# Another loading order at the opening of a Hymba step: three tiles of x, all first weights into idle HGRN tiles, then the other x

## Chip, core and metric

One NeuronCore of a Trainium2 chip runs the whole program. The metric is the device time of one execution in microseconds, as a median of several runs; lower is better. TensorE (PE) does matrix products and transposes, VectorE (DVE), ScalarE (ACT) and GpSimd (POOL) elementwise work, and SyncE (SP) issues most transfers; ACT and POOL issue some of them too.

## The reference

One step of a hybrid decoder layer, for a prompt of 1024 tokens and 8 sample tokens that share all weights. Both groups are normalised and multiplied by one wide input projection; its columns feed sparse attention (NSA: compressed, selected and window branches) and an HGRN2 recurrence, and an output projection follows. What matters here is the first part:

```python
def _rmsnorm(x, g):
    x32 = x.astype(jnp.float32)
    y = x32 * lax.rsqrt(jnp.mean(x32 * x32, axis=-1, keepdims=True) + EPS)
    return (y * g.astype(jnp.float32)).astype(x.dtype)

def _project(x, g_pre, w_in):
    z = _split(_rmsnorm(x, g_pre) @ w_in)          # ..., q_b, f_b, i_b, z_b: 512 columns each
    ...

def _hgrn_inputs(z, lb):
    fl = z['f_b'].astype(f32)
    f = lb + (1.0 - lb) * jax.nn.sigmoid(fl)
    k = (1.0 - lb) * jax.nn.sigmoid(-fl)
    q = jax.nn.silu(z['q_b'].astype(f32))
    v = z['i_b'].astype(f32)
    ...
```

`x_prompt` is 1024 x 1024, `x_sample` 8 x 1024, all in float32. The paged caches are found through a `page_table` of 8 x 8 integers.

## The kernel before

**x.** `load_x` (from L178) brings x in as nine tiles of 128 tokens (the ninth holds the 8 sample tokens), 1024 columns each. They lie in tiles that the HGRN part uses later: tiles 0 to 3 share one buffer `V`, tiles 4 to 8 are `x_in`, in the buffers of `AT`, `S` and `O`. L190 issues all nine loads on SP. For each tile, ACT squares it and sums (L200, `x_sq` and `x_ss`), DVE works out the inverse root by bit tricks and three Newton steps of tiny 128x1 operations (L202 and L79 to L84), DVE scales the tile in place (L214), PE transposes it in two halves of four blocks into PSUM `ph` (L218), and each half is split into a rounded part `xhi` (ACT, L50) and the remainder `xlo` (DVE, L51). The statistics of the next tile are written in the code ahead of the scaling of the present one.

**Weights.** `load_w` (from L224) brings in one block of columns of `w_in` as eight parts of 128 rows. Each part goes by L233 into a raw buffer `w_raw`, of which three cycle; ACT writes the rounded, `g_pre`-scaled part `w_hi` (L238) and DVE the remainder `w_lo` (L239); nine buffers of each. The first block has two pieces of 256 columns, so two loads for a part, 16 in all. From the second block to the fifth, `load_w` also issues, behind the loads, two copies of the window cache in DRAM (L244, 0.5 MB each).

**Products.** PE computes three products for a full-precision one: hi by hi, hi by lo, lo by hi (all at L42). The first block gives the features F, K (ACT at L311 and L312, DVE at L313 and L315) and Q (L323, L324) in groups of 344 tokens: a group needs three tiles of x and all eight weight parts. The second block (L329 evacuates it into `V`, by ACT) has 512 columns; the third is 256 columns wide.

**Small loads.** `gpre` (L290), `hgn` (L141) and two `hg_lo` (L145) are issued by ACT; `hg_lo` is tied behind the last x load. `page_index` loads the page table in eight pieces (L648, `pt_raw`); nothing but the order of the list ties seven of them to a place.

**Order.** The code yields operations and a scheduler of the framework puts them into a list for each engine, by a timeline of its own. Each engine works its list off in order. Each DMA that SP or ACT issues carries one of eight completion semaphores in turn, and waits for the DMA eight before it.

Of the kernel before, what the change touches and what calls it, by code (L numbers as in the profile page):

```python
# [7 lines left out]
F32 = mybir.dt.float32  # L8
# [4 lines left out]
AF = mybir.ActivationFunctionType  # L13
OP = mybir.AluOpType
# [7 lines left out]
TS = T + NB  # L22
D = 1024
EPS = 1e-6
C_Q, C_KC, C_KS, C_KW, C_G, C_ZA, C_QB, C_FB, C_IB, C_ZB = 0, 512, 768, 1024, 1280, 1304, 1816, 2328, 2840, 3352


class Kernel:
# [148 lines left out]
    def load_x(self, ctx):  # L177
        nc, a = self.nc, self.a  # L178
        self.xhi = self.xpool.tile([128, 8, TS], F32R, name="xhi")
        self.xlo = self.xpool.tile([128, 8, TS], F32R, name="xlo")  # L180
        wk = self.pool(ctx, "xwork", bufs=2)
        xs, hp = [], self.hp
        four = hp.tile([128, 8, 512], F32, name="V", bufs=1).rearrange("p a b -> p (a b)")
        for i in range(9):
            n = 128 if i < 8 else NB
            if i < 4:
                x = four[:, i * D:(i + 1) * D]
            else:
                x = hp.tile([128, 8, 128], F32, name="x_in", tag=("AT", "S", "O")[(i - 4) // 2]).rearrange("p a b -> p (a b)")[:n]
            self.xdma = nc.sync.dma_start(x, a["x_prompt"][0, i * 128:i * 128 + n] if i < 8 else a["x_sample"][:, 0])  # L190
            xs.append((i, n, x))

        def norms(tiles):
            ss = wk.tile([128, 4], F32, name="x_ss")
            if tiles[-1] == 8:
                nc.gpsimd.memset(ss, 1.0)
            for j, t in enumerate(tiles):
                _, n, x = xs[t]
                junk = wk.tile([128, D], BF, name="x_sq")[:n]
                nc.scalar.activation(junk, x, AF.Square, accum_out=ss[:n, j:j + 1])  # L200
            ss = ss[:, :len(tiles)]
            nc.vector.tensor_scalar(ss, ss, 1.0 / D, EPS, op0=OP.mult, op1=OP.add)  # L202
            r = wk.tile([128, 4], F32, name="x_rs")[:, :len(tiles)]
            self.rsqrt(wk, r, ss)
            return r

        groups = [(i,) for i in range(9)]
        r = norms(groups[0])
        for gi, tiles in enumerate(groups):
            rn = norms(groups[gi + 1]) if gi + 1 < len(groups) else None  # L210
            for j, t in enumerate(tiles):
                i, n, x = xs[t]
                tok = slice(i * 128, i * 128 + n)
                nc.vector.tensor_scalar(x, x, r[:n, j:j + 1], None, op0=OP.mult)  # L214
                for h in range(2):
                    p = self.ps_h.tile([128, 512], F32, name="ph").rearrange("p (a b) -> p a b", a=4)
                    for k in range(4):
                        nc.tensor.transpose(p[:, k, :n], x[:, (4 * h + k) * 128:(4 * h + k + 1) * 128], self.ident[:n, :n])  # L218
                    self.split(self.xhi[:, 4 * h:4 * h + 4, tok], self.xlo[:, 4 * h:4 * h + 4, tok], p[:, :, :n],
                               nc.scalar, nc.vector)  # L220
            r = rn
            yield gi

    def load_w(self, src, *parts):  # L224

        nc = self.nc
        out = []
        width = sum(p[1] for p in parts)
        for k in range(8):
            raw = self.wpool.tile([128, 512], F32, name="w_raw", bufs=3)[:, :width]  # L230
            o = 0
            for c0, n in parts:
                dma = nc.sync.dma_start(raw[:, o:o + n], src[k * 128:(k + 1) * 128, c0:c0 + n])  # L233
                o += n
            hi = self.wpool.tile([128, 512], F32R, name="w_hi", bufs=9)[:, :width]
            lo = self.wpool.tile([128, 512], F32R, name="w_lo", bufs=9)[:, :width]
            g = self.gpre[:, k:k + 1]
            nc.scalar.activation(hi, raw, AF.Copy, scale=g)  # L238
            nc.vector.scalar_tensor_tensor(lo, raw, g, hi.bitcast(F32), op0=OP.mult, op1=OP.subtract)  # L239
            out.append((hi, lo))  # L240
        self.nload += 1
        for b in range(2 * self.nload - 4, 2 * self.nload - 2):
            if 0 <= b < NB:
                self.after(nc.sync.dma_start(  # L244
                    self.a["win_kv_sample"][0, b, :511].rearrange("s a h d -> s (a h d)"),
                    self.a["cache_win_kv"][0, b, 1:].rearrange("s a h d -> s (a h d)")), dma)
        return out
# [32 lines left out]
    def project(self, ctx):  # L280
        nc, a = self.nc, self.a
# [5 lines left out]
        hp = self.hp = self.pool(hctx, "hg", bufs=2)  # L287
        with ExitStack() as c:
            self.gpre = self.xpool.tile([128, 8], F32, name="gpre")
            nc.scalar.dma_start(self.gpre, a["g_pre"][0].rearrange("(k p) -> p k", p=128))  # L290
            self.nload = 0
            x = self.load_x(c)
            next(x)
            w0 = self.load_w(a["w_in"][0], (C_FB, 256), (C_QB, 256))
            for _ in x:
                pass
            self.consts2(c, mp)
# [5 lines left out]
        K, Q, F = {}, {}, {}  # L303
# [338 lines left out]
    def page_index(self, pool):  # L642

        nc = self.nc
        pt = self.a["page_table"]
        raw = pool.tile([128, NB], I32, name="pt_raw", bufs=1)
        for i in range(8):
            dma = nc.sync.dma_start(raw[16 * i:16 * i + 16], bass.AP(tensor=pt.tensor, offset=pt.offset + i, ap=[[0, 16], [8, NB]]))  # L648
            if i == 0:
                self.pidma = dma  # L650
        lane = pool.tile([128, NB], I32, name="pt_lane", bufs=1)
        nc.gpsimd.iota(lane, pattern=[[0, NB]], base=0, channel_multiplier=1)
        nc.vector.tensor_scalar(lane, lane, 15, None, op0=OP.bitwise_and)
        self.pidx = self.cp.tile([128, NB], I32, name="pidx")
        nc.vector.scalar_tensor_tensor(self.pidx, raw, 16.0, lane, op0=OP.mult, op1=OP.add)
# [738 lines left out]
```

## Time and profile before

| | us |
|---|---|
| median of 3 runs | 1093.54 |
| lowest, highest run | 1088.66, 1094.07 |
| profiled execution, its own time | 1092.95 |
| its span in the trace | 1091.2 |
| PE busy | 1051.9 |
| DVE, ACT, POOL busy | 618.0, 388.5, 241.1 |

Starts and lengths in the trace count from the start of the span. PE's busy time overlaps with its own weight loads (PEld). An engine's row says in square brackets, or behind the last bar, how long it idled ahead and what ended that. ACTq and SPq are the queues of transfers that these engines issue; a row of them covers from the first issue to the end of the last. The first product of this kernel starts after 20 us, and the stage of the first block ends at about 77 us.

### The profile page before, as it was taken

What the parts mean: (1) busy time and instruction counts of PE and PEld (TensorE: products, weight loads), DVE (VectorE), ACT (ScalarE), POOL (GpSimd) and SP (SyncE); (2) the same over time, 40 slices, a digit from 0 to 9 for tenths busy, and PEclk for the clock granted to TensorE, in tenths of its full rate; (3) what the DMA queues carried; (4) which work ended last, traced back from release to release, by engine and by line L of the source; (5) the groups of instructions that cost most, each with busy time, mean ns of one, the idle gap of its engine ahead of it and who ended that gap; (6) DMA issues with size and microseconds to landing.
All of it is one profiled execution on the core that took longest, in us unless ns stands there. A gap on an engine that the chain in (4) does not pass through costs nothing.

```text
span 1091.2 us, 18921 instructions
## 1 busy us (share of the span) xinstructions
PE 1051.9 (96%) x7021; PEld 936.8 (86%) x7021; DVE 618.0 (57%) x1822; ACT 388.5 (36%) x786; POOL 241.1 (22%) x276
## 2 busy tenths in 40 slices
PE   4999999999899899999989999999999999999998
PEld 3898799999789899999968898888788888778876
DVE  6847565666484535543574666766655677461223
ACT  4622234313133335432224544553554332241112
POOL 0024231331031133002023111111323133131111
PEclk9999999999999999999969999999999999999999
DMA  6212023333454666304468711001831474131110
GB/s 195 78 29 68 11 72 100 117 101 120 144 173 135 193 222 208 135 1 118 123 186 250 189 38 42 20 21 41 230 111 42 137 199 119 41 97 49 47 37 31
DMA packets 119007, 116.44 MB, mean 107 GB/s; under 512 B 18902, under 2 KB 101166, under 8 KB 116612
## 3 DMA queue, kind: packets, MB, share of 16 engines
q1 hardware_dynamic: 97412, 79.46, 25.6%
q10 hardware_dynamic: 19200, 19.01, 5.1%
q0 software_dynamic: 2304, 16.78, 4.6%
q8 instruction: 55, 0.90, 0.4%
q14 instruction: 36, 0.29, 0.1%
HBM read 84.84 MB, written 29.31 MB: 105 GB/s over the span
## 4 chain that ended last, share of the span: by engine, by line
PE 81%; DMA 9%; DVE 5%; issue 2%; ACT 1%; POOL 1%; SPq 0%; ACTq 0%; DVEq 0%; POOLq 0%
PE pa L42 37%; PE pb L42 27%; PE ph L42 9%; PE pt L42 4%; DMA vb<-v_d 2%; DMA w_raw<-w_in 2%; PE ph L714 1%; DMA w1r<-cmp_w 1%; DMA fw_raw<-w_out 1%; PE pa L1124 1%; DMA f_z<-oT_d 1%; DMA cg<-cache_cmp_kv,pidx 1%; DMA V<-x_prompt 1%; PE ph L1318 1%; DVE w_lo L239 1%
## 5 line engine op out<-in xcount | busy, mean ns | idle before, releaser
L42 PEld LDWEIGHTS pb<-V,P 128*128 128x128 f32 x1056 | 143.8, 194 | 11.8 <-POOL P L959 0.9
L42 PE MATMUL pb<-V,P 128*128 128x128 f32 x1056 | 149.2, 279 | 0.5 <-DVE mx L908 0.4
L42 PE MATMUL pa<-xhi,w_hi 128*128 128x344 f32 x384 | 125.7, 329 | 3.3 <-ACT w_hi L238 1.7
L42 PE MATMUL pa<-xlo,w_hi 128*128 128x344 f32 x384 | 124.2, 325 | 0.0
L42 PE MATMUL pa<-xhi,w_lo 128*128 128x344 f32 x384 | 123.3, 326 | 0.0
L954 ACT ACTIVATE P<-ph 128x512 f32<-128x512 f32 (+4 forms) x148 | 85.8, 595 | 100.4 <-PE ph L42 78.3
L915 DVE CUSTOM_DVE_ANT_0 junk<-pa,mask 128x320 bf16<-128x320 f32 (+5 forms) x150 | 73.1, 496 | 35.7 <-PE pa L42 35.1
L42 PE MATMUL pa<-w_lo,xhi 128*128 128x256 f32 (+2 forms) x256 | 79.8, 316 | 0.1
L42 PE MATMUL pa<-w_hi,xlo 128*128 128x256 f32 (+2 forms) x256 | 79.6, 315 | 0.0
L42 PE MATMUL pa<-w_hi,xhi 128*128 128x256 f32 (+2 forms) x256 | 78.9, 317 | 0.0
L42 PEld LDWEIGHTS pa<-xhi,w_hi 128*128 128x128 f32 x384 | 73.3, 191 | 5.0 <-ACT w_hi L238 2.4
L238 ACT ACTIVATE w_hi<-w_raw,gpre 128x512 fp32r<-128x512 f32 (+2 forms) x80 | 47.4, 616 | 78.1 <-DMA w_raw<-w_in 46.5
L42 PEld LDWEIGHTS pa<-xlo,w_hi 128*128 128x128 f32 x384 | 73.2, 191 | 0.1
L42 PEld LDWEIGHTS pa<-xhi,w_lo 128*128 128x128 f32 x384 | 72.7, 190 | 0.4 <-DVE w_lo L239 0.2
L42 PE MATMUL ph<-QA,KA 128*128 128x512 f32 (+4 forms) x148 | 66.4, 451 | 2.5 <-ACT P L954 2.5
L42 PE MATMUL pa<-KB,QB 65*128 65x320 f32 (+6 forms) x195 | 64.8, 369 | 1.1 <-DVE mx L915 0.7
L239 DVE SCALAR_TENSOR_TENSOR w_lo<-w_raw,gpre,w_hi 128x512 fp32r<-128x512 f32 (+2 forms) x80 | 51.4, 663 | 21.6 <-ACT w_hi L238 20.9
L42 PE MATMUL pa<-fw_hi,yh 128*128 128x512 f32 (+1 forms) x160 | 61.7, 385 | 0.0
L42 PE MATMUL pa<-fw_hi,yl 128*128 128x512 f32 (+1 forms) x160 | 61.6, 385 | 0.0
L42 PE MATMUL pa<-fw_lo,yh 128*128 128x512 f32 (+1 forms) x160 | 61.6, 385 | 0.0
L42 PE MATMUL ph<-QB,KB 68*128 68x512 f32 (+3 forms) x148 | 58.5, 405 | 0.0
L42 PE MATMUL pb<-x,w1h 128*128 128x384 f32 (+1 forms) x192 | 55.9, 353 | 0.3 <-ACT x L50 0.3
(457 smaller groups left out, 2391.3 us busy)
## 6 DMA issues: line engine op xcount, KB each, us to landing
w_raw<-w_in SPq DMA_DIRECT2D x32, 256.0 KB
w_raw<-w_in SPq DMA_DIRECT2D x48, 128.0 KB
VS<-sg SPq DMA_DIRECT2D x8, 512.0 KB
sg<-cache_win_kv SPq DMA_DIRECT2D x16, 256.0 KB
fw_raw<-w_out SPq DMA_DIRECT2D x16, 256.0 KB
fw_raw<-ple_gate SPq DMA_DIRECT2D x16, 256.0 KB
f_x<-x_prompt SPq DMA_DIRECT2D x8, 512.0 KB
win_kv_sample<-cache_win_kv SPq DMA_DIRECT2D x8, 511.0 KB
```

The costliest lines, as they stand in the source:

```text
L42: return self.nc.tensor.matmul(out, lhsT, rhs, start=start, stop=stop, skip_group_check=True)
L238: nc.scalar.activation(hi, raw, AF.Copy, scale=g)
L239: nc.vector.scalar_tensor_tensor(lo, raw, g, hi.bitcast(F32), op0=OP.mult, op1=OP.subtract)
L714: nc.tensor.transpose(pt[:, i * 128:(i + 1) * 128], src[b0 + j // 2, kv][:, j % 2, 2 * jp:2 * jp + 2].rearrange("p j d -> p (j d)"), self. ...
L915: nc.vector.tensor_tensor_reduce(junk, pm, mk, 1.0, -1e30, op0=OP.add, op1=OP.max, accum_out=o)
L954: nc.scalar.activation(P, ps, AF.Exp, scale=0.125)
L1124: nc.tensor.transpose(pt[:, j * 128:(j + 1) * 128], rows(j), self.ident)
L1318: nc.tensor.transpose(pt[:, c], h[:, k * 128:(k + 1) * 128], self.ident[:n, :n])
```

## The change

Four edits, all at the opening. The loads: SP issues x tiles 0 to 2, then all 16 pieces of the first weights, then x tiles 3 to 8 (a `yield` in `load_x`). The first weights no longer go through the three raw buffers, but into eight halves of four tiles `w0`, in the buffers of F and K, which are not used until the first products are evacuated. The norms: tiles 1 and 2 share one chain of tiny operations, 128x2 instead of twice 128x1. GpSimd: parts 5 to 7 of the first weights are scaled by POOL in place, copied to `w_hi` by ACT (L50), and subtracted by POOL (L51); DVE and ACT at L247 and L248 do parts 0 to 4 as before. The page table: its loads are tied behind the last weight load issued so far, which is that of the second block.

```diff
@@ load_x
             else:
                 x = hp.tile([128, 8, 128], F32, name="x_in", tag=("AT", "S", "O")[(i - 4) // 2]).rearrange("p a b -> p (a b)")[:n]
+            if i == 3:
+                yield
             self.xdma = nc.sync.dma_start(x, a["x_prompt"][0, i * 128:i * 128 + n] if i < 8 else a["x_sample"][:, 0])
...
-        groups = [(i,) for i in range(9)]
+        groups = [(0,), (1, 2)] + [(i,) for i in range(3, 9)]
@@ load_w
-    def load_w(self, src, *parts):
+    def load_w(self, src, *parts, raws=None):
...
-            raw = self.wpool.tile([128, 512], F32, name="w_raw", bufs=3)[:, :width]
-            o = 0
-            for c0, n in parts:
-                dma = nc.sync.dma_start(raw[:, o:o + n], src[k * 128:(k + 1) * 128, c0:c0 + n])
-                o += n
+            if raws:
+                raw = raws[k]
+            else:
+                raw = self.wpool.tile([128, 512], F32, name="w_raw", bufs=3)[:, :width]
+                o = 0
+                for c0, n in parts:
+                    dma = self.lastw = nc.sync.dma_start(raw[:, o:o + n], src[k * 128:(k + 1) * 128, c0:c0 + n])
+                    o += n
...
-            nc.scalar.activation(hi, raw, AF.Copy, scale=g)
-            nc.vector.scalar_tensor_tensor(lo, raw, g, hi.bitcast(F32), op0=OP.mult, op1=OP.subtract)
+            if raws and k > 4:
+                nc.gpsimd.tensor_scalar(raw, raw, g, None, op0=OP.mult)
+                self.split(hi, lo, raw, nc.scalar, nc.gpsimd)
+            else:
+                nc.scalar.activation(hi, raw, AF.Copy, scale=g)
+                nc.vector.scalar_tensor_tensor(lo, raw, g, hi.bitcast(F32), op0=OP.mult, op1=OP.subtract)
@@ project
             next(x)
-            w0 = self.load_w(a["w_in"][0], (C_FB, 256), (C_QB, 256))
+
+            raws = []
+            for tag in ("F", "F", "K", "K"):
+                t = hp.tile([128, TS], F32, name="w0", tag=tag)
+                raws += [t[:, :512], t[:, 512:1024]]
+            for k, raw in enumerate(raws):
+                for o, c0 in ((0, C_FB), (256, C_QB)):
+                    nc.sync.dma_start(raw[:, o:o + 256], a["w_in"][0, k * 128:(k + 1) * 128, c0:c0 + 256])
+            for _ in range(2):
+                next(x)
+            w0 = self.load_w(None, (C_FB, 256), (C_QB, 256), raws=raws)
             for _ in x:
                 pass
@@ page_index
             dma = nc.sync.dma_start(raw[16 * i:16 * i + 16], bass.AP(tensor=pt.tensor, offset=pt.offset + i, ap=[[0, 16], [8, NB]]))
+            self.after(dma, self.lastw)
```

The scheduler moves more than the diff says. First the list of SP at the opening. `V_126` is the buffer of x tiles 0 to 3, `x_in_131` (before) and `x_in_151` (after) are tile 4, the `x_in` behind them tiles 5 to 7; `w0_130` to `w0_133` each hold two parts of the first weights. Before:

```order
L190 DMA V_126<-x_prompt 128x1024 x4
L190 DMA x_in_131<-x_prompt 128x1024
L190 DMA x_in_133<-x_prompt 128x1024
L190 DMA x_in_135<-x_prompt 128x1024
L190 DMA x_in_137<-x_prompt 128x1024
L190 DMA x_in_139<-x_sample 8x1024
L233 DMA w_raw_192<-w_in 128x256 x2
L233 DMA w_raw_199<-w_in 128x256 x2
L233 DMA w_raw_206<-w_in 128x256 x2
L648 DMA pt_raw_1476<-page_table 16x8x1 x7
L233 DMA w_raw_213<-w_in 128x256 x2
```

And SP at the same place after:

```order
L192 DMA V_126<-x_prompt 128x1024 x3
L310 DMA w0_130<-w_in 128x256 x4
L310 DMA w0_131<-w_in 128x256 x4
L310 DMA w0_132<-w_in 128x256 x4
L310 DMA w0_133<-w_in 128x256 x4
L192 DMA V_126<-x_prompt 128x1024
L192 DMA x_in_151<-x_prompt 128x1024
L192 DMA x_in_153<-x_prompt 128x1024
L192 DMA x_in_155<-x_prompt 128x1024
L192 DMA x_in_157<-x_prompt 128x1024
L192 DMA x_in_159<-x_sample 8x1024
L238 DMA w_raw_1180<-w_in 128x512
```

The loads of x tiles 3 and 4 stand behind sixteen weight loads now; the page table has left the place.

Second, ACT's list from the first `xhi` copies on. A PSUM tile `ph` is half a tile of x: before, `ph_178` and `ph_185` are tile 0, `ph_267` and `ph_274` tile 1, `ph_300` tile 2; `x_in_131` and `x_in_133` are tiles 4 and 5. Before:

```order
L50 CAST xhi_121<-ph_178 128x4x128
L50 CAST xhi_121<-ph_185 128x4x128
L50 CAST xhi_121<-ph_267 128x4x128
L200 ACTIVATE x_sq_315,x_ss_314<-x_in_131 128x1024
L50 CAST xhi_121<-ph_274 128x4x128
L238 ACTIVATE w_hi_195<-w_raw_192,gpre_119 128x512
L200 ACTIVATE x_sq_348,x_ss_347<-x_in_133 128x1024
L150 ACTIVATE hg_ex_510<-hg_ex_510 128x8
L238 ACTIVATE w_hi_202<-w_raw_199,gpre_119 128x512
L50 CAST xhi_121<-ph_300 128x4x128
```

After, from the second half of tile 0 on: `ph_207` is tile 0, `ph_233` and `ph_240` are tile 1, `ph_248` is tile 2; `V_126` in the fourth row is tile 3, `x_in_151` tile 4.

```order
L50 CAST xhi_121<-ph_207 128x4x128
L50 CAST w_hi_282<-w0_132 128x512
L145 DMA hg_lo_488<-hg_lower 128x4x1
L202 ACTIVATE x_sq_215,x_ss_214<-V_126 128x1024
L145 DMA hg_lo_488<-hg_lower 128x4x1
L50 CAST w_hi_287<-w0_133 128x512
L202 ACTIVATE x_sq_298,x_ss_297<-x_in_151 128x1024
L50 CAST xhi_121<-ph_233 128x4x128
L50 CAST w_hi_292<-w0_133 128x512
L50 CAST xhi_121<-ph_240 128x4x128
L50 CAST xhi_121<-ph_248 128x4x128
```

The squares of tiles 3 and 4 stand ahead of all `xhi` copies of tiles 1 and 2 now; before, the square of tile 3 stood ahead of them too, but that of tile 4 behind the first. DVE's list has the same turn: the statistics of tile 4 (`x_ss_297`) stand ahead of the first `xlo` of tile 1.

Third, SP where the loads of the second block end and those of the third (128x256) begin. Before:

```order
L233 DMA w_raw_1233<-w_in 128x512
L233 DMA w_raw_1239<-w_in 128x512
L244 DMA win_kv_sample<-cache_win_kv 16x8176 x2
L233 DMA w_raw_1699<-w_in 128x256
L233 DMA w_raw_1705<-w_in 128x256
```

After:

```order
L238 DMA w_raw_1216<-w_in 128x512
L238 DMA w_raw_1222<-w_in 128x512
L253 DMA win_kv_sample<-cache_win_kv 16x8176 x2
L667 DMA pt_raw_1459<-page_table 16x8x1 x7
L238 DMA w_raw_1682<-w_in 128x256
L238 DMA w_raw_1688<-w_in 128x256
```

Seven loads of the page table stand between the copies of the cache and the third block's first load now, and with eight semaphores in turn that load shares one with the second copy. Elsewhere the lists are those of before but for a few swaps of neighbours.

## Rows read from the trace of the kernel before

**Rows 1.** The page's first part: busy us (share of the span) and instructions.

```profile
PE 1051.9 (96%) x7021; PEld 936.8 (86%) x7021; DVE 618.0 (57%) x1822; ACT 388.5 (36%) x786; POOL 241.1 (22%) x276
```

**Rows 2.** Busy us (instructions) by stretch: PE, PEld, DVE, ACT, POOL; clock, DMA share, GB/s.

```profile
10.40:21.00 10.60, 6.16 (x24) 4.54 (x24) 8.74 (x46) 8.22 (x17) 0.00 (x0) 1.00 0.76 229
21.00:33.00 12.00, 10.12 (x50) 9.09 (x50) 6.98 (x29) 4.29 (x8) 0.00 (x0) 1.00 0.39 109
33.00:77.20 44.20, 43.75 (x286) 42.83 (x287) 26.66 (x85) 19.55 (x40) 6.33 (x9) 1.00 0.11 28
```

**Rows 3.** PE's waits up to 77.2 us: total us, times, longest.

```profile
PE ph L218 <- DVE V L214: 10.4, 1, 10.4
...
PE pa L42 <- ACT w_hi L238: 1.7, 1, 1.7
...
PE pa L42 <- ACT K L312: 0.4, 1, 0.4
```

**Rows 4.** PE's instructions up to 32.95 us: busy, mean ns; idle before and its releasers.

```profile
L42 PE MATMUL pa<-xhi,w_hi 128*128 128x344 f32 x14 | 5.3, 407 | 2.7 <-ACT w_hi L238 1.7 <-ACT xhi L50 1.0
```

**Rows 5.** Timeline of ACT and PE to 33 us: start, length, what [idle before].

```profile
4.39 1.06 ACT L200 ACTIVATE x_sq<-V 128x1024 bf16<-128x1024 f32 x1 [1.57 <-DMA V<-x_prompt]
5.35 0.18 ACT L200 ACTIVATION_READ_ACCUMULATOR x_sq<-V 128x1 f32 x1
...
7.99 2.82 ACTq L145 DMA_DIRECT2D hg_lo<-hg_lower  x2
...
10.40 1.97 PE L218 MATMUL ph<-ident,V 128*128 128x128 f32 x8 [10.40 <-DVE V L214]
...
28.05 0.72 ACT L238 ACTIVATE w_hi<-w_raw,gpre 128x512 fp32r<-128x512 f32 x1 [5.96 <-DMA w_raw<-w_in]
```

**Rows 6.** Timeline of SP's queue to 21 us.

```profile
9.15 7.77 SPq L233 DMA_DIRECT2D w_raw<-w_in  x6
16.97 3.27 SPq L648 DMA_DIRECT2D pt_raw<-page_table  x7
```

**Rows 7.** Waits of SP's queue to 21 us: total, times, longest.

```profile
SPq L190 <- DMA gpre<-g_pre: 2.0, 1, 2.0
```

**Rows 8.** Two stretches of 1 us; columns as in rows 2.

```profile
9.00:10.00 1.00, 0.00 (x0) 0.00 (x0) 1.00 (x8) 0.00 (x0) 0.00 (x0) 1.00 1.03 422
27.00:28.00 1.00, 0.11 (x1) 0.00 (x0) 0.00 (x0) 0.00 (x0) 0.00 (x0) 1.00 1.08 375
```

**Rows 9.** Groups by shape to 60 us; columns as in rows 4.

```profile
L51 DVE TENSOR_TENSOR xlo<-ph,xhi 128x512 fp32r<-128x512 f32 x16 | 10.9, 684 | 2.0 <-ACT xhi L50 1.9
...
L50 ACT CAST xhi<-ph 128x512 fp32r<-128x512 f32 x16 | 9.1, 581 | 4.3 <-PE ph L218 4.2
```

**Rows 10.** Timeline of POOL and of DVE, 40 to 46 us.

```profile
41.72 0.95 POOL L477 MEMSET AT<- 128x1024 f32 x1 [0.34 <-PE ph L218]
...
41.82 1.40 DVE L214 TENSOR_SCALAR x_in<-x_in,x_rs 128x1024 f32<-128x1024 f32 x1
...
44.65 0.75 DVE L214 TENSOR_SCALAR x_in<-x_in,x_rs 128x1024 f32<-128x1024 f32 x1
```

**Rows 11.** POOL's groups in the whole span; columns as in rows 4.

```profile
L51 POOL TENSOR_TENSOR w1l<-w1r,w1h 128x512 fp32r<-128x512 f32 x8 | 10.3, 1296 | 9.3 <-ACT w1h L50 9.3
```

**Rows 12.** Timelines of SP's queue, ACT and PE, 80 to 97 us.

```profile
85.74 6.57 SPq L233 DMA_DIRECT2D w_raw<-w_in  x4
...
90.92 0.51 ACT L238 ACTIVATE w_hi<-w_raw,gpre 128x256 fp32r<-128x256 f32 x1 [3.72 <-DMA w_raw<-w_in]
91.34 1.05 ACT L329 COPY V<-pa 128x512 f32<-128x512 f32 x2
...
94.80 0.39 PE L42 MATMUL pa<-w_hi,xhi 128*128 128x512 f32 x1
```

**Rows 13.** The chain that ended last, in order of time: start, length, what.

```profile
352.14 8.89 DMA vb<-v_d
```

**Rows 14.** A later stretch; columns as in rows 2.

```profile
547.00:568.00 21.00, 17.99 (x67) 12.59 (x67) 15.79 (x76) 5.29 (x9) 4.92 (x13) 0.51 0.69 229
```

## The prediction

> **What bounds the kernel now.** I read the page's busy shares first: TensorE (PE) is busy 1051.9 of 1091.2 us [rows 1], so only its waits and its slow stretches can be won. Then the busy time by stretches: PE is busy for 6.16 of the 10.60 us to 21.00, for 10.12 of the next 12.00, and from 33.00 to 77.20 it stands still for 0.45 us in all [rows 2]. So the opening is the place that the edits reach. Its waits by cause: 10.4 us for the first scaled tile of x, 1.7 for a weight, 0.4 for the evacuation `K` [rows 3]. Up to 33.00 PE has done 24 + 50 = 74 instructions [rows 2], of which 3 x 14 = 42 are products of 344 columns [rows 4] and 32 transposes; what is left of this stage ends at 77.2. The weights are late because three raw buffers cycle: ScalarE (ACT) waits 5.96 us for one of them before 28.05 [rows 5]. This is the wait that the change aims at.
>
> **Part 1, the loads.** All 16 first weight loads leave before x tile 3 (tiles count from 0). Seven issues took SP 3.27 us, so (3.27 - 0.43) / 6 = 0.47 us each, the last one's 0.43 taken off [rows 6]. A DMA also carries one of eight completion semaphores in turn and waits for the DMA eight before it: SP stood 2.0 us for `gpre`, whose semaphore the seventh x load shares [rows 7]. New order: three x from 0.81, three weight parts until 3.6; the fourth part needs gpre. In the old order SP had issued six x tiles by then (0.81 + 6 x 0.5 = 3.8) and went on at 5.8; I take that moment over. Four parts go by 7.4; the next shares its semaphore with tile 2, which held the old queue until 9.15 [rows 6]. Nine more at 0.47 end at 13.3, and only then tile 3 is issued. Tile 0 took 3.5 us, from 0.81 to its square at 4.39 [rows 5], on an empty queue; so tile 3 is there at 16.8 and tile 4, 524 KB behind at 422 GB/s [rows 8], at 18.05. In the old order tile 3 was there by 10.4: the second of the two `hg_lo` issues, 7.99 to 10.81, waited for it [rows 5]. Lower bound: SP is not held, 19 issues at 0.47, tile 3 at 13.3. Upper bound: weight parts moved at 375 GB/s in one stretch, but all loads between 10.4 and 21 at a mean of 229 [rows 2, 8]; 2.1 MB at that rate behind the first three tiles (1.57 MB, through by 8 to 9) end at 17.5, tile 4 at 20.5. I take 16.8 and 18.05, since the 375 is the row with nothing but such parts in it.
>
> **Part 2, ACT and VectorE (DVE) in the new order.** The operations are those of the old kernel: square about 1.2 with its read-out, `w_hi` 0.72, transposes eight in 1.97 [rows 5], `xhi` 0.58, `xlo` 0.68 [rows 9], scaling 0.75 [rows 10]. ACT after tile 2, at 9.1: square 10.3, four `w_hi` 13.2, `xhi`, `w_hi`, `xhi`, a copy `w_hi` (as long as `xhi`), one DMA issue: 16.1. There the order puts the square of tile 3, so ACT waits for the load until 16.8. Then 1.2 + 0.47 + 0.58 = 19.05, the square of tile 4 until 20.25, and only then the first `xhi` of tile 1. DVE has the same knot: the statistics of tile 4 stand ahead of the `xlo` of tile 1. So: small operations and `xhi` 20.9, `xlo` 21.5, four transposes 22.5, `xhi` of tile 2 at 23.1: the first product. DVE meanwhile: `xlo` 22.6, six small ones 23.2, scaling of tile 3 23.95, `xlo` of tile 2 24.65. PE's next product follows four transposes, 0.6 to 1.0 us: about 25.45.
> The joint norm of tiles 1 and 2 saves a chain of tiny DVE operations and puts tile 0's scaling behind tile 2's square, about 11 instead of 9.6; its `xhi` copies are done by 15.5, four microseconds ahead of the knot, so this costs nothing; without that cover it would be 1.5 us.
>
> **Part 3, weights on GpSimd (POOL).** Three scalings and three subtractions of 128x512. The subtraction has a row, 1.30 [rows 11]; the scaling has none: bounds 0.48 (half a clearing of 1024 columns, 0.95, no input [rows 10]) and 1.30 (two inputs); I take 1.0, nearer to the row with inputs. Loads 5 to 7 land from 13 to 15, so scalings end at 16.1, and the last subtraction 1.3 after the last `w_hi` (21.4): 22.7. PE reaches their products after 30. Seven microseconds hide it even at the high bound; DVE is freed of three `w_lo`.
> But POOL is then at work beside DVE. A scaling of x took 1.40 while POOL cleared a tile, and 0.75 alone [rows 10]. The last subtraction can lie beside tile 3's scaling, so I allow 0 to 0.65 there and take 0.3. By the Trainium skill, GPSIMD Engine Reference, section 8 (Key points), GpSimd shares its SBUF interfaces with VectorE and contends with VectorE instructions in a two-port mode or with two SBUF inputs. The trace agrees, 1.40 against 0.75 us; by that rule alone the whole 0.65 is paid, and the sum below ends 0.35 later.
>
> **The sum.** PE goes on in one piece from 25.75. From 33.00 on 286 instructions took 43.75 us, 0.153 each; from 21 to 33 it was 10.12 / 50 = 0.20 [rows 2]. The next 46 products and 8 transposes cost 54 x 0.153 = 8.3, and the slow start 20 x 0.05 = 1.0: 35.05. Against the state at 33.00, 7 products and 4 transposes more are done, 1.7 us; the rest is 44.20 - 0.45 - 1.7 = 42.05, since the wait for `K` has microseconds of cover in the new order. The stage ends at 77.1 instead of 77.2: 0.1 us gained. With tile 4 at its late bound it ends at 79.5, 2.3 lost; the early bound is the first rival.
>
> **Part 4, the page-table loads** leave the opening, where they kept SP for 3.27 us [rows 6] that weights waited behind, and stand behind the second weights and two cache copies, at 85.5. Three find their semaphores free; the last waits for the first copy, and the next weight load for the second. In the old order that load went out at 85.74 and landed 5.2 us later behind the copies' bytes; ACT took it at 90.92 and evacuated two PSUM tiles from 91.34 on; PE starts the product that needs the first of these at 94.80 [rows 12]. New: copies at about 90, load at 92.3, `w_hi` and evacuation until 93.3: 1.5 us of cover left, so nothing. Lower bound 0; upper bound in the second rival.
> What follows has the order of before, but for a few swaps that no wait stands at; its waits hang on PE's own progress and move with it.
> The profiled execution took 1092.95, its span and 1.75 us around it, 0.6 below the median of the three runs. 1092.95 - 0.1 is **1092.8**.
>
> **The rivals.**
> First, the change does what it says: tiles 3 and 4 come in time. Then ACT's own work bounds it: 12.8 us of operations from 9.1 to the first product, 21.9 instead of 23.1: 1.2 less, with no contention 1.5, so 1091.3. For: ACT is then busy throughout. Against: SP is held for gpre and tile 2 as before.
> Second, slower: the weight load behind the cache copies. ACT evacuates nothing until it lands. It decides from a landing at 93.8 (94.80 less `w_hi` 0.43 and evacuation 0.59). The slowest landing of a load from SP's queue in the chain of waits is 8.89 us [rows 13]; a copy like that ends at 93.8, the load at 96.4, a stall of 2.6 us. PE can come out of waits at the lower rate: granted 0.51 of full speed, 1.2 instead of 2.4 GHz, from 547 to 568 [rows 14]. With 2 us for that: 1097.4. For: two new waits on copies. Against: the copies' 1 MB was through in some 4.5 us.
> Third, the stretch at 547 changes, though no edit touches it: three runs of one kernel lie 5.4 us apart. Without its 21 us at half rate up to 10 us less (1083), with a short one more, some 4 (1097).
>
> **How the numbers follow.** Forecast 0.57 (own range 1090 to 1096: the bounds above and the spread of the runs), first rival 0.20, second 0.12, third 0.11 (0.07 down, 0.04 up). About 0.5%, 5.5 us, is what a measurement can tell from no change. Faster by more: 0.06 of the third and 0.03 of the first on top of a low run, 0.09. Slower by more: the tails of the second and third, 0.08. Same 0.83. The range 1088.5 to 1097.4 leaves out the third rival downward and the second's tail.
>
> **What would show it.** In the profile after: no wait of ACT for a weight before 30 us, but one for the x load before the square of tile 3; the first 344-column product near 23, PE in one piece from about 25.7, no wait for `K`. Wrong if the first product comes by 20 (tile 4 was not the knot) or after 26 (loads slower than 229 GB/s), or if ACT idles over 5 us before the 256-column `w_hi` near 92 and PE stands still behind it.

## The result, and the profile after

The changed kernel takes 1101.45 us, a median of 14 runs (1095.71 to 1109.51), beside 1093.61 for the kernel before in the same runs: a ratio of 1.0087, interval 1.0057 to 1.0116. It is 7.8 us slower; forecast was no change. The profiled execution took 1102.93 us, its span 1101.2.

Two places were forecast to decide, and the change's time was lost at the second. First the opening, the same stretches as [rows 2], and one that follows them:

```profile
10.40:21.00 10.60, 3.91 (x16) 3.13 (x16) 10.13 (x25) 7.06 (x13) 7.36 (x5) 1.00 0.96 312
21.00:33.00 12.00, 10.15 (x55) 9.37 (x56) 11.38 (x63) 7.66 (x16) 1.79 (x3) 1.00 0.41 128
33.00:77.20 44.20, 44.20 (x293) 43.62 (x292) 22.05 (x63) 15.78 (x34) 6.06 (x8) 1.00 0.03 7
77.20:120.00 42.80, 38.91 (x170) 31.45 (x169) 28.11 (x35) 9.85 (x15) 16.10 (x10) 0.96 0.19 56
```

Up to 77.2 PE has done 16 + 55 + 293 instructions instead of 24 + 50 + 286 in [rows 2], so it is four ahead: the opening is even. The loss is in the last row: 3.89 us without work, and a mean clock of 0.96. PE's waits to 100 us (total, times, longest), which answer to [rows 3]:

```profile
PE ph L220 <- DVE V L216: 16.2, 2, 10.7
PE pa L42 <- ACT V L348: 3.9, 1, 3.9
PE ph L220 <- DVE xlo L51: 2.7, 2, 2.4
```

The wait for a weight and that for `K` of [rows 3] are gone, as the change meant; a wait for `V`, the evacuation of the second block, is new (the kernel before has no wait between 77 and 100 us). What is behind it, in the timelines of SP's queue, ACT and PE, where [rows 12] had 85.74, 90.92 and 94.80:

```profile
85.15 4.01 SPq L667 DMA_DIRECT2D pt_raw<-page_table  x7
90.18 8.70 SPq L238 DMA_DIRECT2D w_raw<-w_in  x4
...
97.50 0.51 ACT L247 ACTIVATE w_hi<-w_raw,gpre 128x256 fp32r<-128x256 f32 x1 [10.68 <-DMA w_raw<-w_in]
97.92 1.05 ACT L348 COPY V<-pa 128x512 f32<-128x512 f32 x2
...
98.53 0.50 PE L42 MATMUL pa<-w_hi,xhi 128*128 128x512 f32 x1 [3.89 <-ACT V L348]
```

ACT stands for 10.68 us before a 256-column weight, the two evacuations queue behind it, and PE waits. This is a sign that the prediction itself had named for being wrong: ACT idle for over 5 us before this weight, with PE standing still behind it. The chain of waits names the two transfers that end last there:

```profile
84.54 5.58 DMA win_kv_sample<-cache_win_kv
...
90.18 7.29 DMA w_raw<-w_in
```

The load left at 90.18, when the second copy of the window cache had landed, and then took 7.29 us for 128 KB. The stretches tell what the transfers did in that time (columns as in [rows 2]):

```profile
85.00:90.00 5.00, 5.00 (x23) 4.07 (x22) 4.76 (x8) 0.73 (x1) 2.01 (x1) 1.00 0.75 245
90.00:95.00 5.00, 4.64 (x21) 3.44 (x19) 0.69 (x1) 0.00 (x0) 0.29 (x1) 1.00 0.05 0
95.00:98.00 3.00, 0.00 (x0) 0.00 (x0) 0.00 (x0) 0.50 (x2) 0.00 (x0) 1.00 0.41 131
98.00:103.00 5.00, 4.47 (x13) 3.51 (x14) 1.48 (x3) 3.02 (x6) 2.38 (x1) 0.66 0.10 26
```

From 90 to 95 us hardly any bytes move, though a load of 128 KB is in the queue: the 16 DMA engines are busy for 0.05 of the time on average. The share alone does not say how many of them are at work. The trace has 470 packets from 90.5 to 94.5 us, all under 512 bytes; each is some 8 ns long, and about half of them start before the one ahead has ended, so more than one engine moves them. And after the stall PE's granted clock is 0.66 on average to 103 us, so between its two levels: part of the stretch went at 1.2 GHz instead of 2.4, which costs (1 - 0.66) x 5 = 1.7 us. Together with 3.89 that makes 5.6, nearly the whole step of 5.7 us that follows here.

To follow such steps, each TensorE instruction of one trace was paired with the same one of the trace before, and the differences of their starts taken, as a median over 20 us. This offset tells where a kernel stands against the one before; below it is called the lead (negative) or the lag. The changed kernel has a lead of 0.32 us at 60 to 80 us, a lag of 5.38 from 100 on and of 10.0 at the end.

### The profile page after: what moved, and what is told of

The parts are those of the page before. It is cut to its first block, busy times and chain, and to the rows that moved or that the text cites. A ratio compares the mean times of both kernels' runs of the same rounds, so it can differ in the third digit from the quotient of the medians.

```text
span 1101.2 us, 18906 instructions
## 1 busy us (share of the span) xinstructions
PE 1052.2 (96%) x7021; PEld 937.2 (85%) x7021; DVE 620.6 (56%) x1807; ACT 388.5 (35%) x786; POOL 249.3 (23%) x282
## 4 chain that ended last, share of the span: by engine, by line
PE 78%; DMA 10%; DVE 6%; issue 3%; ACT 1%; POOL 1%; SPq 1%; ACTq 0%; DVEq 0%; POOLq 0%
PE pa L42 35%; PE pb L42 26%; PE ph L42 9%; PE pt L42 4%; DMA vb<-v_d 2%; DMA w_raw<-w_in 2%; PE ph L734 1%; DMA V<-x_prompt 1%; DMA w1r<-cmp_w 1%; PE pa L1144 1%; DMA fw_raw<-w_out 1%; DMA fw_raw<-ple_gate 1%; DMA cg<-cache_cmp_kv,pidx 1%; DVE fw_lo L51 1%; DVE w_lo L248 1%
## 5 line engine op out<-in xcount | busy, mean ns | idle before, releaser
L247 ACT ACTIVATE w_hi<-w_raw,gpre 128x512 fp32r<-128x512 f32 (+2 forms) x72 | 41.7, 604 | 78.7 <-DMA w_raw<-w_in 46.8
L248 DVE SCALAR_TENSOR_TENSOR w_lo<-w_raw,gpre,w_hi 128x512 fp32r<-128x512 f32 (+2 forms) x72 | 46.7, 672 | 24.3 <-ACT w_hi L247 23.3
```

## The experiments

Two theories of the stall were put against each other. A: the seven page-table loads hold SP's queue, since each moves 128 pieces of 4 bytes; what stands behind them waits. B, as the prediction's second rival had it: the weight load shares a semaphore with the second cache copy and so leaves late. For the opening the question was which of the other three edits does what. Offsets and the start of the first 344-column product come from one trace each, and all offsets are taken against the same trace of the kernel before; medians and ratios from 10 to 14 runs beside runs of the kernel before.

| kernel | first product, us | offset at 60 to 80 us | at 120 us | median, us | before, us | ratio, interval |
|---|---|---|---|---|---|---|
| before | 21.04 | 0 | 0 | | | |
| the change | 24.73 | -0.32 | 5.38 | 1101.45 | 1093.61 | 1.0087, 1.0057 to 1.0116 |
| e14, the change again | 25.59 | 1.03 | 6.44 | 1102.80 | 1095.15 | 1.0078, 1.0057 to 1.0099 |
| e1, before with the table moved | 20.99 | -2.98 | 3.68 | 1098.99 | 1094.86 | 1.0046, 1.0018 to 1.0073 |
| e2, change with the table behind x | 25.27 | 0.34 | 0.32 | 1096.88 | 1094.86 | 1.0029, 1.0004 to 1.0054 |
| e3, four table loads in place of seven | 25.86 | 2.05 | 2.69 | 1098.45 | 1094.86 | 1.0037, 1.0003 to 1.0072 |
| e4, table in 32-byte rows | 26.13 | 0.85 | 0.83 | 1096.88 | 1094.86 | 1.0033, 1.0000 to 1.0067 |
| e5, before with the table mid-block | 20.90 | -3.46 | -3.46 | 1092.24 | 1094.09 | 0.9978, 0.9955 to 1.0001 |
| e6, e2 without GpSimd | 29.22 | 4.16 | 4.14 | 1102.11 | 1094.09 | 1.0060, 1.0035 to 1.0085 |
| e7, e2 with single norms | 24.11 | 0.80 | 0.78 | 1098.80 | 1094.09 | 1.0030, 0.9999 to 1.0061 |
| e8, e2 with all x first | 21.26 | -0.98 | -0.98 | 1097.52 | 1094.09 | 1.0017, 0.9986 to 1.0048 |
| e9, idle tiles alone | 20.75 | -3.68 | -3.68 | 1094.05 | 1093.54 | 1.0013, 0.9986 to 1.0039 |
| e10, e9 with three x first | 28.18 | 4.74 | 4.72 | 1100.07 | 1093.54 | 1.0072, 1.0047 to 1.0096 |
| e11, e5 with the joint norm | 20.00 | -4.70 | -4.70 | 1092.08 | 1093.54 | 0.9977, 0.9947 to 1.0008 |
| e12, e5 with GpSimd | 20.36 | 2.81 | 2.81 | 1099.33 | 1093.54 | 1.0057, 1.0036 to 1.0078 |
| e13, e9 with the joint norm | 21.32 | -1.94 | -1.94 | 1095.56 | 1095.15 | 1.0004, 0.9983 to 1.0026 |

### e1: the kernel before, with the table moved alone

```diff
-                dma = nc.sync.dma_start(raw[:, o:o + n], src[k * 128:(k + 1) * 128, c0:c0 + n])
+                dma = self.lastw = nc.sync.dma_start(raw[:, o:o + n], src[k * 128:(k + 1) * 128, c0:c0 + n])
...
             dma = nc.sync.dma_start(raw[16 * i:16 * i + 16], ...)
+            self.after(dma, self.lastw)
```

> The kernel before with one edit: its seven page-table loads are tied behind the second block's weights, as in the change; every other engine's order is that of before. Both theories of the stall (A: the 4-byte packets of the page table hold SP's queue for 8 to 10 us; B: the next weight load waits for the semaphore of the second cache copy) expect the wait of ACT for the first 256-column weight to grow from 3.7 to about 10 us and PE to stand 3 to 5 us near 94 and then at the lower clock for some 4 us, 5 to 6 us in all. At the opening A expects the 5.96 us wait of ACT for a weight before 28 us to fall under 2 us, and the stage to end at 75 to 76 instead of 77.2; B (a weight waits there for raw buffers) expects that wait to stay above 4 us and the stage to end at 77. Time: A 1097 to 1099, B 1099 to 1100, before 1093.6.

One edit, only SP's order differs, and it has both faces. At the opening it gives a lead of 2.98 us: ACT's 5.96 us wait [rows 5] is gone. Near 92 us it costs 6.66. The stall (of PE's waits) and the stretch before it:

```profile
PE pa L42 <- ACT V L329: 4.0, 1, 4.0
```

```profile
87.00:92.40 5.40, 4.98 (x22) 3.73 (x20) 0.81 (x2) 0.00 (x0) 0.63 (x1) 1.00 0.06 1
92.40:95.00 2.60, 0.00 (x0) 0.00 (x0) 0.00 (x0) 0.03 (x1) 0.00 (x0) 0.88 0.46 147
```

So the move of the table is enough for the stall. The opening speaks against B, under which it should not have changed. It doesn't tell A from a third reading, that the seven issues take 3.27 us of SP's time [rows 6]; the trace before does. The next weight loads were issued from 20.36 us on, and the same stillness stands there, up to 26:

```profile
20.00:26.00 6.00, 5.00 (x21) 4.64 (x21) 3.78 (x19) 2.08 (x4) 0.00 (x0) 1.00 0.05 1
26.00:28.00 2.00, 1.11 (x8) 0.83 (x6) 0.00 (x0) 0.00 (x0) 0.00 (x0) 1.00 0.85 281
```

### e2: the change, with the table behind x

```diff
-            self.after(dma, self.lastw)
+            self.after(dma, self.xdma)
```

> The changed kernel with one edit undone: the page-table loads are tied behind the last x load, so SP issues them after the third load of the second block; all other orders are those of the changed kernel. Both theories: no stall of PE near 94, the first 256-column weight scaled before 92, full clock from 92 to 112. Stage of the first block ends at 77 as with the change. If the move of the page table is the whole loss: 1092 to 1095. If the other three edits bear part of it through the rest of the program (the trace after loses another 4 us in small steps from 238 us on): 1096 to 1098.

SP's queue and ACT, where the change had 90.18 and 97.50:

```profile
86.07 6.36 SPq L238 DMA_DIRECT2D w_raw<-w_in  x4
...
90.86 0.51 ACT L247 ACTIVATE w_hi<-w_raw,gpre 128x256 fp32r<-128x256 f32 x1 [3.36 <-DMA w_raw<-w_in]
```

The stall is gone and the offset stays at 0.3, as both theories had it: the move of the table makes the stall. The median is 2.0 us over that of before, the ratio 3.2 (0.4 to 5.9 by the interval), in the range that was written for a part borne by the other edits. The trace, whose offset is 0.83 at the end, doesn't show where such a part would lie; but it is of the fastest of the twelve runs (1093.73), so it can't rule the part out.

### e3 and e4: A against B

```diff
-            self.after(dma, self.lastw)
+            self.after(dma, self.lastw if i > 3 else self.xdma)
```

> The changed kernel, but only four of the seven page-table loads stand behind the cache copies, three behind x; so the next weight load shares its semaphore with a weight load that landed long ago. B (semaphore): the load leaves near 87.5 and the first 256-column weight is scaled by 91; no stall. A (4-byte packets, about 1.4 us for each load): the queue is held from 85.1 for 4 x 1.4 = 5.7 us, the weight lands at 92 to 94, a stall of 0 to 0.5 us. Time 1092 to 1096 by both.

```diff
-            dma = nc.sync.dma_start(raw[16 * i:16 * i + 16], bass.AP(..., offset=pt.offset + i, ap=[[0, 16], [8, NB]]))
+            dma = nc.sync.dma_start(raw[16 * i:16 * i + 16], bass.AP(..., offset=pt.offset + 8 * i, ap=[[0, 16], [1, NB]]))
```

> The changed kernel, all seven page-table loads where the change puts them, but each reads one row of the table (16 packets of 32 bytes instead of 128 of 4 bytes), so the sample's pages are gathered in another order than the reference's. The issues, semaphores and waits are those of the changed kernel. B (semaphore of the second copy): the load still leaves at 90.2 and lands at 97.5, PE stands 3.9 us, 1101. A (4-byte packets): the load leaves at 90.2 at the latest and lands within 2.5 us, by 92.7; no stall or under 0.5 us; 1092 to 1096.

SP's queue and ACT of e3, then of e4:

```profile
87.52 2.05 SPq L667 DMA_DIRECT2D pt_raw<-page_table  x4
89.68 8.09 SPq L238 DMA_DIRECT2D w_raw<-w_in  x4
...
96.38 0.51 ACT L247 ACTIVATE w_hi<-w_raw,gpre 128x256 fp32r<-128x256 f32 x1 [7.19 <-DMA w_raw<-w_in]
```

```profile
86.34 3.94 SPq L667 DMA_DIRECT2D pt_raw<-page_table  x7
91.22 3.51 SPq L238 DMA_DIRECT2D w_raw<-w_in  x4
...
93.35 0.51 ACT L247 ACTIVATE w_hi<-w_raw,gpre 128x256 fp32r<-128x256 f32 x1 [5.30 <-DMA w_raw<-w_in]
```

e4 reads rows of the table instead of columns, so the sample's pages are gathered in another order than the reference's; its operations and their order are those of the change. In e3 the load shares no semaphore with a copy, leaves right behind the fourth table load, and still needs 96.38 - 89.68 = 6.7 us; B had it leave near 87.5 and scaled by 91, in 3.5. In e4 every issue and wait of the change is there, the load leaves as late as 91.22, and is there 2.1 us later; PE does not stand still. Only the pieces differ, 16 of 32 bytes instead of 128 of 4 bytes for each load; number and size change together, and no run separates them. B falls, and so does SP's time for the seven issues, 3.94 us here too; A stands: the semaphore's wait (4.4 us of late issue) is under the cover that the prediction gave it, the 4-byte pieces are not. A's figure was low for e3 (the weight was expected at 92 to 94 and came at 96.38; 2 us of that are this execution's later opening), and its stall of 0.4 us is the one expected. Both kernels took longer than was written for A, 1098.45 and 1096.88 instead of 1092 to 1096.

### e5: the kernel before, with the table mid-block

```diff
+                dma = nc.sync.dma_start(...); self.lastw = dma if k < 3 else self.lastw
...
+            self.after(dma, self.lastw)
```

> The kernel before with the page-table loads moved, not behind all the weights of the second block but behind its third one; every other engine's order is that of before. A (the 4-byte packets hold SP's queue for some 10 us wherever they stand, and it matters only who is behind): the opening loses its 6 us wait of ACT, the first block's stage ends 3.0 us earlier, at 74.2 as with the tie alone, the first 256-column weight is scaled 2 to 3 us ahead of its time and nothing stands still near 94; 3 us under before, 1091 to 1093 beside 1094.9. Rival (the gain of the opening is given back where the products of the second block wait for its last weights): a wait of PE for a weight of 1 to 4 us at 74 to 80; 1093 to 1096.

A's expectation held: lead 3.46 at 60 us, kept past 94. PE's waits up to 100 us, all of them ahead of 21 us:

```profile
PE ph L218 <- DVE V L214: 10.5, 1, 10.5
PE ph L218 <- DVE xlo L51: 3.2, 2, 2.2
PE pa L42 <- ACT xhi L50: 1.0, 1, 1.0
```

With the table away the three raw buffers don't hold PE up. 1092.24 beside 1094.09 is the best that was found (with e11), though its interval touches 1.

### e6 to e8: e2, with one of the other three edits undone

```diff
-            if raws and k > 4:
+            if raws and k > 7:                                  # e6
...
-        groups = [(0,), (1, 2)] + [(i,) for i in range(3, 9)]
+        groups = [(i,) for i in range(9)]                       # e7
...
-            if i == 3:
+            if i == 99:                                         # e8, with one next(x) less ahead of load_w
```

> The changed kernel with the page table behind x (as in the run before) and without GpSimd's part: ACT and DVE make all eight weight parts. If POOL's contention with DVE (two scalings of x took 1.8 to 2.1 us instead of 1.5, a 128x1 operation 1.2 us instead of 0.15, ACT waits 1.2 us for a part scaled by POOL) sets the opening: the stage of the first block ends 1 to 2 us earlier, 75.5 to 76.5. If tile 3's landing (18.0 to 19.4 us in four traces) sets it, as the prediction said: 77 to 78, unchanged within 0.7.

> The changed kernel with the page table behind x and with a chain of tiny operations for each tile, as before, instead of one for tiles 1 and 2; the first half of tile 1 then stands ahead of tile 3's square in ACT's list. If the joint norm together with the squares of tiles 3 and 4 is what holds tiles 1 and 2 (second transposes at 18 us instead of 15): transposes of tile 1 by 15, first product by 23.5 instead of 24.7 to 26, stage end 75.5 to 76.5. If tile 3's landing sets it: no change within 0.7, 77 to 78.

> The changed kernel with the page table behind x and with all nine x loads ahead of the first weights, as before; the weights still go into the idle tiles, GpSimd and the joint norm stay. If x tiles 3 and 4 behind sixteen weight loads are the knot, as the prediction said: no wait of ACT for an x load after 13 us, first product by 22, stage end 74 to 75, 1091 to 1093. If POOL and the joint norm are: first product after 23, stage end 76 to 78.

Without GpSimd the opening is 3.8 us later, against both expectations. Its three `w_lo` go to DVE, whose list then waits twice on late x loads, for the square of tile 3 and for `hg_lo`, which is tied behind the last x load:

```profile
20.14 0.15 DVE L204 TENSOR_SCALAR x_ss<-x_ss 128x1 f32<-128x1 f32 x1 [2.33 <-ACT x_sq L202]
...
20.98 1.42 DVE L216 TENSOR_SCALAR V<-V,x_rs 128x1024 f32<-128x1024 f32 x2
...
27.57 0.16 DVE L147 TENSOR_TENSOR hg_mx<-hg_lo 128x4 f32<-128x4 f32 x1 [2.26 <-DMA hg_lo<-hg_lower]
```

The first stands ahead of the last steps of the chain for tiles 1 and 2, the second ahead of the `xlo` of tile 1. So GpSimd's part helps in this order, although it also costs. Single norms change little (0.80 for 0.34; five traces of the change's loading order spread from -0.3 to 2.1). All x first gains 1.3 us in the trace beside e2's, as the knot at tile 3 was to do, but not the 2 to 3 us that were expected for it; against the five traces it is 0.7 to 3.0, and the median shows no gain (1097.52, where 1091 to 1093 was written, beside 1096.88 for e2).

### e9 to e13: the parts alone, and two of them together

e9 is e2 with the edits of e6, e7 and e8 together, so that of the change the idle tiles alone stay. The others:

```diff
-            if i == 99:
+            if i == 3:                                          # e10, on e9
...
-        groups = [(i,) for i in range(9)]
+        groups = [(0,), (1, 2)] + [(i,) for i in range(3, 9)]   # e11 on e5, e13 on e9
...
+            if self.nload == 0 and k > 4:                       # e12, on e5
+                nc.gpsimd.tensor_scalar(raw, raw, g, None, op0=OP.mult)
+                self.split(hi, lo, raw, nc.scalar, nc.gpsimd)
+            else:
```

> Of the change's edits only the weights into idle tiles, with all nine x loads ahead of them, no joint norm, nothing on GpSimd; the page table behind x. In DVE's list the scalings and xlo of tiles 0 to 2 stand ahead of all but four w_lo. If what costs at the opening is work on weights ahead of work on x: second transposes by 15.5, first product at 20.5 to 22, stage of the first block ends 2.5 to 3.5 us before that of the kernel before (73.7 to 74.7), 1091 to 1094. If the idle tiles as such cost (weights moved in one piece beside x): first product after 23, stage end 76 or later.

> The same as the run with the idle tiles alone, but three x tiles first, then the weights, then the other x, as in the change. All eight w_lo stand ahead of the first xlo of tile 1 in DVE's list, and tile 1's second half behind them. If work on weights ahead of x is what costs: second transposes at 17 or later, first product 25 to 28, stage end 77 to 80, 3 to 6 us later than with x first. If tile 3's late landing is what costs, and the three-tiles-first order alone brings tiles 1 and 2 no harm: first product by 23.5, stage end by 76.

> The kernel before with the page table behind the third load of the second block, and the joint norm of tiles 1 and 2 as the only other edit. Prediction's step (costs nothing under cover, 1.5 us without): here there is no knot to cover it, so the second transposes come at 16 to 17 instead of 14.7, the first product 1 to 1.5 us later, stage end 75 to 75.5 instead of 73.7. Rival (nine tiny operations of 0.15 us less on a busy DVE): first product up to 1 us earlier, stage end 73 to 73.7.

> The kernel before with the page table behind the third load of the second block, and parts 5 to 7 of the first weights on GpSimd as the only other edit (out of the three raw buffers). PE waits for no weight after 21 us in that kernel, so DVE's three w_lo less buy nothing: stage end 73.7 within 0.7. If GpSimd's scaling, 1.6 us each, delays the parts on the path, or its contention slows DVE's work on tiles 3 and 4: stage end 74.5 to 76, PE waiting for a weight at 25 to 30.

> The change without the two parts that cost most when tried alone: all nine x loads ahead of the weights, nothing on GpSimd; the weights in the idle tiles and the joint norm stay, the page table behind x. If the parts add up (idle tiles alone ended the first block's stage 3.7 us ahead of the kernel before, the joint norm alone took another 1.2 off): first product by 20.2, stage end 4.5 to 5.2 us ahead, 72.0 to 72.7; 1090 to 1092. If the parts don't add (the lists are made anew for each kernel): stage end anywhere from 73 to 76.

The idle tiles alone give nothing beyond e5 (3.68 for 3.46): what the three raw buffers were blamed for was the table's doing. Three x tiles first costs 8.4 us beside e9 (3 to 6 was expected; 6.0 by the medians), the largest price of any part. The timelines of DVE, e9 and then e10, show why; L248 is a `w_lo`, L51 an `xlo`:

```profile
12.30 0.75 DVE L216 TENSOR_SCALAR V<-V,x_rs 128x1024 f32<-128x1024 f32 x1
13.86 0.69 DVE L51 TENSOR_TENSOR xlo<-ph,xhi 128x512 fp32r<-128x512 f32 x1
...
19.22 0.75 DVE L248 SCALAR_TENSOR_TENSOR w_lo<-w,gpre,w_hi 128x512 fp32r<-128x512 f32 x1
```

```profile
17.05 1.41 DVE L248 SCALAR_TENSOR_TENSOR w_lo<-w,gpre,w_hi 128x512 fp32r<-128x512 f32 x2
...
18.44 0.75 DVE L248 SCALAR_TENSOR_TENSOR w_lo<-w,gpre,w_hi 128x512 fp32r<-128x512 f32 x1
19.10 0.69 DVE L51 TENSOR_TENSOR xlo<-ph,xhi 128x512 fp32r<-128x512 f32 x1
```

In e9 the first `w_lo` comes at 19.22, behind the scalings of four tiles; in e10 eight of them, some 5.5 us of DVE, are done before the `xlo` of tile 1 at 19.10. Weights that arrive early are worked on early, and DVE's work on x, which the first product needs, stands behind them: the transposes of tile 2 start at 23.32, where e9 had 17.53. Another 1.6 us of the 7.4 by which the first product is late come from ACT's list: the `xhi` of tile 2 (27.56) stands there behind a second-block weight and an operation that waits for the `hg_lo` load, and PE waits 2.92 us for it, where e9 had 0.99.

The joint norm alone gains 1.2 us, the rival's side, by one trace each; the medians of e11 and e5 (1092.08, 1092.24) don't show it. GpSimd alone costs 6.3 (7.1 by the medians), over the 0.8 to 2.3 of its rival. POOL and DVE at the place (timeline, e12), and PE, which waits for the result:

```profile
30.57 2.53 POOL L51 TENSOR_TENSOR w_lo<-w_raw,w_hi 128x512 fp32r<-128x512 f32 x2
...
30.62 1.25 DVE L83 SCALAR_TENSOR_TENSOR rs_t<-rs_t,x_ss 128x1 f32<-128x1 f32 x1
...
31.91 1.21 DVE L84 SCALAR_TENSOR_TENSOR rs_g<-rs_t,rs_g 128x1 f32<-128x1 f32 x1
...
34.53 1.50 DVE L214 TENSOR_SCALAR x_in<-x_in,x_rs 128x1024 f32<-128x1024 f32 x1
...
36.75 0.44 PE L218 MATMUL ph<-ident,x_in 128*128 128x128 f32 x2 [2.35 <-DVE xlo L51]
```

Operations of 128x1 with two inputs (L83, L84), 0.15 us elsewhere, end only with POOL's subtraction beside which they start. Two shorter waits of PE (0.72 and 0.95 us) follow, and then the lower clock again (0.72 of full speed on average from 44 to 48 us).

The parts don't add: e13, idle tiles and joint norm, leads by 1.94, where 3.68 and 1.24 would make 4.9. Each kernel gets new lists from the scheduler, and a part's price is that of the list it stands in.

### e14: the change again

> The changed kernel itself, for a second trace. The first one stands 5.4 us behind the kernel before at 100 us and another 4.6 us at the end, in steps at 240, 440, 560, 780 and 975 us. If these steps belong to the change: again a stall of 3.5 to 4.5 us near 94, 5 to 7 us behind at 100 us, and again 3.5 to 6 us more from there to the end, at the same places. If they belong to the single execution (low-clock stretches that come and go): the stall and the 5 to 7 us again, but steps elsewhere, from -4 to +5 us in sum. Opening -0.5 to +2, since tile 3 landed at 18.0 to 19.4 in four traces of this order.

The stall comes back (3.6 us; the weight is scaled at 98.56), and so does the lag at 120 us, 6.44. The steps after it do not: from 220 to 400 us this trace gains 4.7 us on the kernel before, where the first one lost 1.1, and from there to 460 it loses 3.3, where the first lost 1.5; at the end it is 8.4 behind, the first 10.0. So the later steps differ from one execution of this kernel to the next; most of them can't be laid to the change.

## Why the prediction was wrong, point by point

**Part 4, the page-table loads: the term that failed.** Its working put their price at SP's time, 3.27 us [rows 6], and let the next weight load land some 2 us after the copies, at 92.3. The copies ended when it said (about 90; 90.12), the load left when the second copy had landed, as it said (90.18), and the cover was what it said: the load was 97.5 - 92.3 = 5.2 us late against that working, cover 1.5, which makes 3.7, and PE stood for 3.89. The one wrong number is the load's own time, 7.29 instead of some 2. A price for 4-byte pieces in the queue is missing from the whole text. The trace before had it: 6 us at 0.05 and 1 GB/s behind the seven issues (shown with e1). The forecast read the 5.96 us wait [rows 5] as three buffers cycling; e9 gives that cause 0.2 us, e5 gives the table 3.5, by one trace each.

**The second rival was right in place and consequence and wrong in its condition.** It had a stall at this product, 2.6 us, and 2 for the lower clock; 3.9 and 1.8 came. But it hung on a copy as slow as 8.89 us [rows 13], and so had a chance of 0.12. The copy took 5.58.

**The sum of the opening was right for wrong reasons.** Forecast 0.1 ahead; 0.32 ahead in one trace, 1.03 behind in the other. Seen by parts, taking the table away gains 3 to 3.5 (e1, e5), and the other three edits together give that back (e2 against e5: 3.8). The forecast had neither term.

**Part 1, the loads.** Tile 3 issued at 12.68 (forecast 13.3), its square started at 17.98 (16.8), within the bounds; ACT waited 2.09 us for it, and the statistics of tiles 3 and 4 did stand ahead of tile 1:

```profile
17.98 1.06 ACT L202 ACTIVATE x_sq<-V 128x1024 bf16<-128x1024 f32 x1 [2.09 <-DMA V<-x_prompt]
...
19.55 1.05 ACT L202 ACTIVATE x_sq<-x_in 128x1024 bf16<-128x1024 f32 x1
...
20.60 0.56 ACT L50 CAST xhi<-ph 128x512 fp32r<-128x512 f32 x1
```

The upper bound for tile 4, 20.5, doesn't follow from the rate it names: two tiles of 524 KB at 229 GB/s behind 17.5 would end at 22.1; nothing hung on it, since its square (19.55) did not wait for the load. The knot is real and worth 1.3 us by e8's trace, near the 1.2 that the first rival gave it. The first product came at 24.73 instead of 23.1, since DVE was late by itself too: the forecast counted DVE's work from 20.9 on, and left out the five `w_lo` ahead of tiles 1 and 2, whose transposes came at 18.18.

**Part 2's joint norm, "costs nothing"**: gains 1.2 alone by the traces, about nothing in the change (e7). **Part 3, GpSimd.** The scaling took 1.62 us each; both bounds, 0.48 and 1.30, were too low. PE did not wait for these parts, as said. Contention was put at 0.3, upper end 0.65. The two scalings of x beside it took 2.10 and, without GpSimd in e6, 1.42: 0.68. The sentence of the Trainium skill (GPSIMD Engine Reference, section 8, Key points) by which GpSimd contends with VectorE instructions in a two-port mode or with two SBUF inputs agrees with that, as far as it goes; it gives no size. Of the small operations beside POOL's subtractions three took 1.20, 0.64 and 0.48 us instead of 0.15, for which no term stood:

```profile
16.94 2.10 DVE L216 TENSOR_SCALAR V<-V,x_rs 128x1024 f32<-128x1024 f32 x2
...
20.24 1.20 DVE L83 SCALAR_TENSOR_TENSOR rs_t<-rs_t,x_ss 128x1 f32<-128x1 f32 x1
```

**What stays open.** The median moved by 7.8 and 7.7 us, the offset at 120 us is 5.4 and 6.4. The same holds for every row of the table: the median moved further to the slow side than the offset at 120 us says, by 0.5 to 4.4 us, 2.4 on average. So the leads of e5, e9, e11 and e13 (1.9 to 4.7 us) don't arrive whole in the medians: -1.9, +0.5, -1.5 and +0.4. One trace of the kernel before stands behind all offsets. If its first 120 us were some 2 us slower than usual, that would look just like this, and the gains at the opening that are counted against it would be smaller by as much; it may also be that the kernels lose more behind 120 us. No run decides this. The price of the stall does not hang on it, since it is a step within one trace (5.7 us in the change, 6.7 in e1, 5.4 in e14), and the medians of the change and of e2 lie 4.6 us apart, the ratios 6.

## What to carry to other kernels

Price a transfer by what it does to the queue, not by the time of its issue: look in the trace for stretches in which the DMA engines stand at a few hundredths of their time and no bytes move, and see which load ended just before. Tiny loads belong where the issuing queue waits anyway, or in fewer and larger pieces. And before weights are brought in early, see which engine will work on them, and what of the first product's chain then stands behind that work in its list.

## What the runs showed of the hardware

Loads of 4-byte pieces: seven of them (896 pieces, 3.5 KB) held SP's queue for 9 to 10 us from their first issue, with 0.05 of the DMA engines' time in use and no bytes of the load behind them moving; as 112 pieces of 32 bytes the same seven issues held nothing. In the changed kernel 470 packets of some 8 ns were recorded in 4 us, and they overlap. An estimate from that, if the 16 engines share them evenly, which the trace does not tell by engine: each moves one in 0.14 us, and works for 8 ns of them. By the Trainium skill (DMA: Bandwidth & Descriptors, section Queues, rings and completion order) descriptors on one DMA engine are consumed in ring order, which agrees with a load that waits behind the pieces on all of them.

A DVE operation of 128x1 that starts beside a two-input subtraction of POOL can take 1.2 us instead of 0.15; those that did have two tensor inputs (L83, L84), and one-input operations beside POOL's first subtraction in the changed kernel (19.16 to 19.69 us) kept to 0.15. And a stall of PE of 3.9 us cost another 1.8 us behind it, since the granted clock was 0.66 of full speed on average in the 5 us that followed.
